# Moving the left operands of three matmul stages to other addresses relative to their weights

## The chip, the cores and the metric

The kernel runs on one core of a Trainium2 chip. The metric is device time in microseconds (us) of one execution. Before the change three runs took 2002.62, 2002.87 and 2003.62 us, median 2002.87.

## The reference

One decoder layer on 256 tokens of width 2048, in float32: half a SwiGLU feed-forward (FFN), a mixer (eight retention heads beside eight gated-delta heads, one input and one output projection), another half FFN, and a final RMSNorm.

```python
x = x + 0.5 * _swiglu(_rmsnorm(x, norm_ffn1_w[l]), ffn1_w_gate[l], ffn1_w_up[l], ffn1_w_down[l])
x = x + _mixer(_rmsnorm(x, norm_mix_w[l]), positions, w_in[l], ..., w_out[l])
x = x + 0.5 * _swiglu(_rmsnorm(x, norm_ffn2_w[l]), ffn2_w_gate[l], ffn2_w_up[l], ffn2_w_down[l])
return _rmsnorm(x, norm_final_w)
```

The weights are 2048 x 5632 (gate, up), 5632 x 2048 (down), 2048 x 8208 (mixer in) and 2048 x 2048 (mixer out).

## The kernel before

All products are done in float32 quality by splitting both operands into a high and a low part (type fp32r) and adding three matmuls, `triple` (lines 144 to 151): left high by weight high, left high by weight low, left low by weight high. A matmul has a stationary left operand of 128 x 128 (`lhsT`, loaded by an LDWEIGHTS) and a moving right operand of 128 x 512, which is the piece of weights. The next LDWEIGHTS runs while the present matmul streams.

Weights come by DMA in pieces of 256 rows x 512 columns (`raw`); ScalarE casts the high part (`whi`, line 135), VectorE subtracts for the low part (`wlo`, line 136). `whi` and `wlo` are pools of four buffers each, used by all stages. The last four pieces of the second FFN have buffers of their own (pool `wlast`, `KEPT` = 4).

The left operands are, by stage:

- gate and up of both FFNs and the mixer's input projection: `xh`, `xl`, the transposed, normalised activations, kept for the whole kernel;
- the down projections of the two FFNs: `hh`, `hl` (lines 327, 328), in a pool that each FFN opens anew. A down projection is done in two halves, of 6 and of 5 blocks of 512 rows;
- the mixer's output projection: four pairs named `m8`, `mh4`/`ml4`, `mh0`/`ml0`, `mh12`/`ml12`, which take over buffers of the pool `gd` (line 476).

The order of the instructions on TensorE (PE), VectorE (DVE) and ScalarE (ACT) is written out by hand. In the mixer, side chains on the same engines (convolutions, gates, the delta rule, retention) are run between the matmuls of the input projection.

The three pools that hold left operands are laid out one behind the other in each partition of SBUF, so a dummy tile at a pool's start shifts all that follows in it. Before the change there are two such pads, of 8 floats (32 bytes): in the first FFN's pool and in `gd`. Every slice that a matmul reads starts at a multiple of 512 bytes behind its tile's start, so a stage has one distance between left operand and weights modulo 256.

Of the kernel before, what the change touches and what calls it, by code (L numbers as in the profile page):

```python
# [13 lines left out]
F32 = mybir.dt.float32  # L14
# [5 lines left out]
P = 128  # L20
# [9 lines left out]
Q = 32  # L30
KEPT = 4
LEAD = 3
PAD = 8
NLEV = 7
HALF = P // 2
LEV0 = 5
# [49 lines left out]
def hybrid_layer(ctx: ExitStack, tc: tile.TileContext, a: dict, out: bass.AP):  # L86
# [99 lines left out]
    def product_units(left, w, rows, c0, sizes=()):  # L186

        accs = [acc.tile([P, NB], F32, name="acc") for _ in range(NT)]

        def units():
            for ks, _ in product_pieces(rows, w, c0, sizes):
                hi, lo = stream.take((w.tensor.name, c0), len(ks))
                for j, k in enumerate(ks):
                    for t in range(NT):
                        triple(accs[t], left, rows[k][0], t, hi[:, j, :], lo[:, j, :], k == 0, k == len(rows) - 1)
                        yield

        return accs, units()

    def staggered_product(left, w, rows, c0, kept):


        accs = [acc.tile([P, NB], F32, name="acc") for _ in range(NT)]
        pieces = list(product_pieces(rows, w, c0))
        split_pieces = {}

        def piece(i, t):  # L210
            if t == 0:
                split_pieces[i] = stream.take((w.tensor.name, c0), len(pieces[i][0]))
            hi, lo = split_pieces[i]
            for j, k in enumerate(pieces[i][0]):
                triple(accs[t], left, rows[k][0], t, hi[:, j, :], lo[:, j, :], k == 0, k == len(rows) - 1)

        lag = 2
        stream.lead = 1
        for i in range(len(pieces)):
            piece(i, 0)  # L220
            if i == 0:
                do_later()
            if lag <= i < len(pieces) - kept:
                piece(i - lag, 1)
        yield accs[0]
        for i in range(len(pieces) - kept - lag, len(pieces)):
            piece(i, 1)
        yield accs[1]
# [13 lines left out]
    def product(*args, every=2):  # L242
        accs, units = product_units(*args)
        beside(units, every)
        return accs
# [4 lines left out]
    def vector_transposed(dst, src):  # L250


        dv = dst.rearrange("p n (t c) -> p t n c", t=NT)
        sv = src.rearrange("p t (n c) -> p t n c", c=P)

        def piece(r):
            for q in range(0, P, Q):
                V.transpose(dv[q:q + Q, :, :, r:r + Q], sv[r:r + Q, :, :, q:q + Q])  # L258

        return [partial(piece, r) for r in range(0, P, Q)]  # L260
# [24 lines left out]
    def norm_block(ssq, i, b, xt=None):  # L285


        kb = NB // P
        ks = range(b * kb, (b + 1) * kb)

        def squares():
            for t in range(NT):
                square_sum(ssq, b, t)

        if xt is None:
            return [partial(norm_pair, i, k) for k in ks[::2]] + [squares]
        return (vector_transposed(xt, x[:, :, b * NB:(b + 1) * NB]) + [partial(norm_tile, i, k, xt[:, k - ks[0], :]) for k in ks]
                + [squares])
# [5 lines left out]
    def row_factor(ssq):  # L304
        w = ssq.shape[1]
        r = small.tile([P, w], F32, name="rms")
        V.tensor_reduce(r, ssq, mybir.AxisListType.X, ALU.add)
        V.tensor_scalar(r, r, 1.0 / D, EPS, ALU.mult, ALU.add)
        q = small.tile([P, w], F32, name="rfac")
        power(q, r, -0.5, w)  # L310
        return q

    def ffn(idx, factor, after, lead=None):


        wg, wu, wd = a[f"ffn{idx}_w_gate"][0], a[f"ffn{idx}_w_up"][0], a[f"ffn{idx}_w_down"][0]
        nblk, nout = FF // NB, D // NB
        halves = [range(0, (nblk + 1) // 2), range((nblk + 1) // 2, nblk)]
        kb = NB // P
        rf = None  # L320
        with (tc.manual_schedule(engines={E.PE, E.DVE, E.Activation}), tc.tile_pool(name=f"ffn{idx}", bufs=1) as hp, tc.tile_pool(name=f"ffe{idx}", bufs=1) as ep,
              tc.tile_pool(name=f"wlast{idx}", bufs=KEPT) as wl):
            pools["last"] = wl
            if idx == 1:

                hp.tile([P, PAD], F32, name="pad")
            hh = hp.tile([P, len(halves[0]) * kb, T], F32R, name="hh")
            hl = hp.tile([P, len(halves[0]) * kb, T], F32R, name="hl")

            def h_left(k):  # L330
                return hh[:, k, :], hl[:, k, :]

            for hf in halves:
                rows = [(k, k) for k in range(KD)]
                for i, b in enumerate(hf):
                    u = None
                    if b == 0 and lead:
                        g, gs = product_units(x_left, wg, rows, 0, (1, 1))
                        u, us = product_units(x_left, wu, rows, 0)
                        for k in range(0, KD, 2):  # L340
                            lead(k, ep)
                            for units in (gs, us):
                                deque(islice(units, 2 * NT), 0)
                            stream.lead = 1
                        stream.lead = LEAD
                    else:
                        g = product(x_left, wg, rows, b * NB)
                    if rf is None:
                        rf = factor()
                    sg = ep.tile([P, NT, NB], F32, name="sg", bufs=4 - idx)  # L350
                    for t in range(NT):
                        S.activation(sg[:, t, :], g[t], AF.Silu, scale=rf[:, t:t + 1])  # L352
                    u = u or product(x_left, wu, rows, b * NB)
                    h = ep.tile([P, NT, NB], F32, name="h", bufs=4 - idx)
                    for t in range(NT):
                        V.scalar_tensor_tensor(h[:, t, :], u[t], rf[:, t:t + 1], sg[:, t, :], ALU.mult, ALU.mult)
                    ht = ep.tile([P, kb, T], F32, name="ht")
                    later.extend(vector_transposed(ht, h))
                    for j in range(0, kb, 2):
                        ks = slice(i * kb + j, i * kb + j + 2)  # L360
                        later.append(partial(split, hh[:, ks, :], hl[:, ks, :], ht[:, j:j + 2, :]))
                r0 = hf[0] * kb
                rows = [(k, r0 + k) for k in range(len(hf) * kb)]
                last = hf is halves[1]
                for b in range(nout):
                    if last and idx == 2 and b == nout - 1:
                        o = staggered_product(h_left, wd, rows, b * NB, KEPT)
                    else:
                        o = product(h_left, wd, rows, b * NB)
                    for t, ot in enumerate(o):  # L370
                        xs = x[:, t, b * NB:(b + 1) * NB]
                        V.scalar_tensor_tensor(xs, ot, 0.5, xs, ALU.mult, ALU.add)
                        if last:
                            after(b, t, ep)
# [93 lines left out]
    def first_factor():  # L468
        for t in range(NT):
            square_sum(ssqs[0], D // NB - 1, t)  # L470
        return row_factor(ssqs[0])

    ffn(1, first_factor, to_mixer, start)


    with tc.manual_schedule(engines={E.PE, E.DVE, E.Activation}), tc.tile_pool(name="gd", bufs=1) as gd:
        gd.tile([P, PAD], F32, name="pad")

        def mixed_out(o, b, xt=None):
            for t in range(NT):  # L480
                xs = x[:, t, b * NB:(b + 1) * NB]
                V.tensor_tensor(xs, o[t], xs, ALU.add)
            later.extend(norm_block(ssqs[2], 2, b, xt))

        env = dict(x_left=x_left, ident=ident, mx=mx, cv=cv, qd=qd, product=product, product_units=product_units, power=power,
                   split=split,
                   weight_piece=weight_piece, do_later=do_later, beside=beside, mixed_out=mixed_out,
                   row_factor=lambda: row_factor(ssqs[1]), params=(cst, alog, dtb, gnw, cw, posi))
        mixer(tc, a, gd, env)
# [659 lines left out]
```

## Time and profile before

| | |
|---|---|
| median of three runs | 2002.87 us |
| the profiled execution | 2002.66 us |
| its span, first to last instruction | 2000.8 us |
| PE busy | 1966.6 us, 98% |
| LDWEIGHTS (PEld) busy | 1618.0 us, 81% |
| DVE busy | 1289.9 us, 64% |
| ACT busy | 892.4 us, 45% |
| granted TensorE clock, mean | 0.997 |

Time outside the span is 1.9 us. A matmul's recorded duration is longer than the distance to the next matmul's start, since matmuls are pipelined: "busy" says that PE has one under way, and the distance from start to start says what one costs. The stages follow each other: first FFN to about 727 us, mixer to about 1272 us, second FFN to the end.

### The profile page before, as it was taken

The numbers are of one execution on the slowest core, as the hardware profiler recorded it, in microseconds if no ns is written. First come the engines' busy times: TensorE is split into PE (matmuls) and PEld (weight loads), VectorE is DVE, ScalarE is ACT, GpSimd is POOL, SyncE is SP. The second block draws the span as 40 slices with busy tenths as digits, with TensorE's granted clock in tenths as the row PEclk, the third lists the DMA queues.
The fourth block names the chain that finished last, engine by engine and source line by source line (L and its number), as shares of the span: only waits on it lengthen the run. The fifth ranks groups of instructions, "written<-read, shape, count | busy, mean of one in ns | idle before, by whom it ended". The sixth has DMA issues, their size and how long they took to land.

```text
span 2000.8 us, 23620 instructions
## 1 busy us (share of the span) xinstructions
PE 1966.6 (98%) x8836; PEld 1618.0 (81%) x8836; DVE 1289.9 (64%) x1818; ACT 892.4 (45%) x1075; POOL 61.8 (3%) x79
## 2 busy tenths in 40 slices
PE   9999999999999999999999999999999999999998
PEld 7888888888888887877777788888888888888886
DVE  5676664457666777676568567766676544677654
ACT  6444443343444456644344334544444334444443
POOL 0000000000000000120121000000000000000000
PEclk9999999999999999999999999999999999999999
DMA  9565655665565565586557835666665656665564
GB/s 313 190 190 180 208 197 193 193 197 182 188 208 193 190 188 169 160 172 162 124 152 170 165 122 184 206 200 194 195 189 179 210 193 196 191 195 182 189 208 139
DMA packets 195267, 373.06 MB, mean 186 GB/s; under 512 B 14544, under 2 KB 15184, under 8 KB 195024
## 3 DMA queue, kind: packets, MB, share of 16 engines
q1 hardware_dynamic: 193888, 368.38, 60.3%
q0 software_dynamic: 832, 1.84, 0.4%
q8 instruction: 69, 1.13, 0.2%
q10 hardware_dynamic: 432, 1.34, 0.2%
q14 instruction: 46, 0.38, 0.1%
HBM read 368.89 MB, written 2.62 MB: 186 GB/s over the span
## 4 chain that ended last, share of the span: by engine, by line
PE 48%; DVE 4%; issue 1%; ACT 1%; DMA 0%; POOLq 0%; DVEq 0%; ACTq 0%
PE acc L149 15%; PE acc L151 15%; PE acc L150 15%; DVE wlo L136 1%; ACT whi L135 1%; PE mx L748 1%; PE qd L828 0%; DVE yn L857 0%; DVE Yb L858 0%; DMA raw<-in_ffn_w_down_dram 0%; DVE rv L1056 0%; PE mx L1025 0%; DVE gu L769 0%; PE mx L979 0%; PE mx L811 0%
## 5 line engine op out<-in xcount | busy, mean ns | idle before, releaser
L136 DVE TENSOR_TENSOR wlo<-raw,whi 128x1024 fp32r<-128x1024 f32 (+1 forms) x689 | 840.4, 1227 | 623.0 <-ACT whi L135 620.1
L135 ACT CAST whi<-raw 128x1024 fp32r<-128x1024 f32 (+1 forms) x689 | 720.3, 1051 | 818.3 <-PE acc L151 741.7
L149 PE MATMUL acc<-whi,xh 128*128 128x512 f32 x1920 | 762.1, 397 | 1.6 <-DVE xl L273 1.6
L150 PE MATMUL acc<-wlo,xh 128*128 128x512 f32 x1920 | 750.3, 391 | 1.2 <-DVE wlo L136 1.2
L151 PE MATMUL acc<-whi,xl 128*128 128x512 f32 x1920 | 750.2, 391 | 0.0
L151 PEld LDWEIGHTS acc<-whi,xl 128*128 128x128 f32 x1920 | 361.6, 188 | 76.2
L149 PEld LDWEIGHTS acc<-whi,xh 128*128 128x128 f32 x1920 | 362.4, 189 | 74.6 <-ACT whi L135 2.7
L150 PEld LDWEIGHTS acc<-wlo,xh 128*128 128x128 f32 x1920 | 362.2, 189 | 74.1 <-DVE wlo L136 3.1
L150 PE MATMUL acc<-wlo,hh 128*128 128x512 f32 x704 | 274.0, 389 | 0.2 <-DVE wlo L136 0.2
L149 PE MATMUL acc<-whi,hh 128*128 128x512 f32 x704 | 273.9, 389 | 0.0
L151 PE MATMUL acc<-whi,hl 128*128 128x512 f32 x704 | 273.9, 389 | 0.0
L258 DVE STREAM_TRANSPOSE ht<-h 32x256 f32<-32x256 f32 x352 | 153.3, 436 | 5.3
L150 PEld LDWEIGHTS acc<-wlo,hh 128*128 128x128 f32 x704 | 132.1, 188 | 28.2 <-DVE wlo L136 0.7
L149 PEld LDWEIGHTS acc<-whi,hh 128*128 128x128 f32 x704 | 132.1, 188 | 27.5
L151 PEld LDWEIGHTS acc<-whi,hl 128*128 128x128 f32 x704 | 132.1, 188 | 27.3
L141 ACT CAST hh<-ht 128x512 fp32r<-128x512 f32 x44 | 27.2, 617 | 121.2 <-DVE ht L258 121.2
L142 DVE TENSOR_TENSOR hl<-ht,hh 128x512 fp32r<-128x512 f32 x44 | 30.3, 688 | 15.1 <-ACT hh L141 15.1
L352 ACT ACTIVATE sg<-acc,rfac 128x512 f32<-128x512 f32 x44 | 29.9, 690 | 19.3 <-PE acc L151 16.6
L149 PE MATMUL acc<-whi,mh 128*128 128x512 f32 x96 | 37.7, 393 | 0.0
L151 PE MATMUL acc<-whi,ml 128*128 128x512 f32 x96 | 37.4, 390 | 0.0
L150 PE MATMUL acc<-wlo,mh 128*128 128x512 f32 x96 | 37.4, 389 | 0.0
L726 DVE SCALAR_TENSOR_TENSOR y<-cv,cw,y 128x255 f32<-128x255 f32 (+2 forms) x72 | 34.6, 480 | 3.0 <-ACT y L718 1.2
(215 smaller groups left out, 762.2 us busy)
## 6 DMA issues: line engine op xcount, KB each, us to landing
raw<-in_ffn_w_up_dram SPq DMA_DIRECT2D x176, 512.0 KB, 4.5
raw<-in_ffn_w_down_dram SPq DMA_DIRECT2D x176, 512.0 KB, 4.6
raw<-in_ffn_w_gate_dram SPq DMA_DIRECT2D x175, 512.0 KB, 4.3
raw<-in_w_in_dram SPq DMA_DIRECT2D x128, 512.0 KB, 4.8
raw<-in_w_out_dram SPq DMA_DIRECT2D x32, 512.0 KB, 3.5
x<-in_x_dram SPq DMA_DIRECT2D x4, 512.0 KB, 6.3
out_dram<-x SPq DMA_DIRECT2D x8, 256.0 KB, 2.4
h<-in_xt_dram SPq DMA_DIRECT2D x7, 256.0 KB, 5.9
```

The source lines that it names most:

```text
L135: S.copy(hi, raw)
L136: V.tensor_tensor(lo, raw, hi.bitcast(F32), ALU.subtract)
L141: S.copy(hi, src)
L142: V.tensor_tensor(lo, src, hi.bitcast(F32), ALU.subtract)
L149: PE.matmul(o, lhsT=sh, rhs=hi, start=first, stop=False)
L150: PE.matmul(o, lhsT=sh, rhs=lo, start=False, stop=False)
L151: PE.matmul(o, lhsT=sl, rhs=hi, start=False, stop=last)
L258: V.transpose(dv[q:q + Q, :, :, r:r + Q], sv[r:r + Q, :, :, q:q + Q])
L352: S.activation(sg[:, t, :], g[t], AF.Silu, scale=rf[:, t:t + 1])
L726: V.scalar_tensor_tensor(yy[:, lag:], pt[:, j, :T - lag], w[:, 3 - lag:4 - lag], yy[:, lag:], ALU.mult, ALU.add)
L748: PE.matmul(pt[:, j, :], lhsT=lhsT, rhs=rhs, start=True, stop=True)
```

## The change

The first FFN's pad grows from 8 to 56 floats, the second FFN gets one of 16 floats, the mixer's is taken out.

```diff
-PAD = 8
...
-            if idx == 1:
-
-                hp.tile([P, PAD], F32, name="pad")
+
+            hp.tile([P, 56 if idx == 1 else 16], F32, name="pad")
             hh = hp.tile([P, len(halves[0]) * kb, T], F32R, name="hh")
...
     with tc.manual_schedule(engines={E.PE, E.DVE, E.Activation}), tc.tile_pool(name="gd", bufs=1) as gd:
-        gd.tile([P, PAD], F32, name="pad")
```

No instruction is added, taken out or moved, and no wait changes: the two programs have the same instructions in the same order with the same semaphores on every engine. Only addresses differ. Byte addresses within a partition, modulo 256:

| tiles | before | after |
|---|---|---|
| `whi`, `wlo`, `xh`, `xl`, `raw`, `x` | 160 | 160 |
| `hh`, `hl`, `h`, `sg`, `ht` of the first FFN | 160 | 96 (64 below the weights) |
| `hh`, `hl`, `h`, `sg`, `ht` of the second FFN | 160 | 224 (192 below, or 64 above) |
| `whi`, `wlo` of the last four pieces | 160 | 224 (as `hh`, `hl`) |
| `m8`, `mh4`, `ml4` and the others; `kq`, `gu`, `kd` and all of `gd` | 160 | 128 (32 below) |
| `rkT`, `rqT`, `sc`, `rv`, `rg` | 32 | 0 |
| `slr` | 0 | 224 |
| `pe`, `y`, `sq` | 224 | 192 |
| `ident` | 128 | 128 |

## Rows read from the trace of the kernel before

**Rows 1.** The page, parts 1 and 2: engines' busy time; granted clock by slice.

```profile
PE 1966.6 (98%) x8836; PEld 1618.0 (81%) x8836; DVE 1289.9 (64%) x1818; ACT 892.4 (45%) x1075; POOL 61.8 (3%) x79
...
PEclk9999999999999999999999999999999999999999
```

**Rows 2.** The page, part 4: the chain that ended last, shares by line.

```profile
PE acc L149 15%; PE acc L151 15%; PE acc L150 15%; DVE wlo L136 1%; ACT whi L135 1%; PE mx L748 1%; PE qd L828 0%; DVE yn L857 0%; DVE Yb L858 0%; DMA raw<-in_ffn_w_down_dram 0%; DVE rv L1056 0%; PE mx L1025 0%; DVE gu L769 0%; PE mx L979 0%; PE mx L811 0%
```

**Rows 3.** Windows: stretch, length, busy (instructions), granted clock, DMA share, GB/s.

```profile
280.00:400.00 120.00, 120.00 (x531) 99.38 (x530) 61.48 (x58) 48.30 (x47) 0.00 (x0) 1.00 0.59 194
...
1680.00:1880.00 200.00, 200.00 (x884) 165.59 (x883) 127.58 (x154) 86.61 (x91) 0.00 (x0) 1.00 0.61 194
```

**Rows 4.** One tile's instructions in a stretch: count, ns min/median/max, first and last start.

```profile
L149 PE MATMUL acc<-whi,hh x192: 389/389/389, 270.4 to 400.3; 128*128 128x512 f32 x192
...
L149 PE MATMUL acc<-whi,xh x320: 389/389/389, 401.0 to 617.9; 128*128 128x512 f32 x160
...
L149 PE MATMUL acc<-whi,hh x192: 389/389/389, 1534.6 to 1664.4; 128*128 128x512 f32 x192
```

**Rows 5.** Groups by line on PE: count, busy us, mean ns, idle before.

```profile
L149 PE MATMUL acc<-whi,hh 128*128 128x512 f32 x704 | 273.9, 389 | 0.0
...
L149 PE MATMUL acc<-whi,mh 128*128 128x512 f32 x96 | 37.7, 393 | 0.0
...
L149 PE MATMUL acc<-whi,m 128*128 128x512 f32 x32 | 12.6, 395 | 0.0
```

**Rows 6.** The page, part 5: the casts that feed the matmuls.

```profile
L136 DVE TENSOR_TENSOR wlo<-raw,whi 128x1024 fp32r<-128x1024 f32 (+1 forms) x689 | 840.4, 1227 | 623.0 <-ACT whi L135 620.1
L135 ACT CAST whi<-raw 128x1024 fp32r<-128x1024 f32 (+1 forms) x689 | 720.3, 1051 | 818.3 <-PE acc L151 741.7
```

**Rows 7.** Timeline in the mixer: start us, us, engine, line, operation.

```profile
805.58 0.14 PEld L716 LDWEIGHTS cv<-ident,pe 128*128 128x128 f32 x1
...
824.91 0.39 PE L151 MATMUL acc<-whi,xl 128*128 128x512 f32 x1
824.92 0.19 PEld L773 LDWEIGHTS mx<-gu,slr 128*128 128x128 f32 x1
825.14 0.40 PE L773 MATMUL mx<-gu,slr 128*128 128x512 f32 x1
...
832.30 0.48 PEld L736 LDWEIGHTS mx<-ident,kq 128*128 128x128 f32 x3
...
843.03 0.41 PEld L811 LDWEIGHTS mx<-kq 128*128 128x128 f32 x2
...
973.41 0.53 PEld L748 LDWEIGHTS mx<-w,kd 128*128 128x128 f32 x3
...
1044.00 0.42 PEld L1034 LDWEIGHTS mx<-rv,sc 128*128 128x128 f32 x2
```

**Rows 8.** The matmul that streams over each of those loads, columns as in rows 4.

```profile
L151 PE MATMUL acc<-whi,xl x1: 392/392/392, 805.6 to 805.6; 128*128 128x512 f32 x1
...
L151 PE MATMUL acc<-whi,xl x1: 391/391/391, 824.9 to 824.9; 128*128 128x512 f32 x1
...
L151 PE MATMUL acc<-whi,xl x1: 392/392/392, 832.3 to 832.3; 128*128 128x512 f32 x1
...
L151 PE MATMUL acc<-whi,xl x1: 389/389/389, 843.0 to 843.0; 128*128 128x512 f32 x1
...
L151 PE MATMUL acc<-whi,xl x1: 389/389/389, 973.4 to 973.4; 128*128 128x512 f32 x1
...
L151 PE MATMUL acc<-whi,xl x1: 392/392/392, 1044.0 to 1044.0; 128*128 128x512 f32 x1
```

**Rows 9.** The tile `slr` in the stretch 1011 to 1012 us, columns as in rows 4.

```profile
L773 PE MATMUL mx<-gu,slr x2: 391/392/393, 1011.4 to 1011.7; 128*128 128x512 f32 x2
```

**Rows 10.** Window of the 32 gate matmuls of 256 columns (tile `wab`), columns as in rows 3.

```profile
738.40:742.10 3.70, 3.67 (x32) 3.37 (x32) 0.00 (x0) 0.00 (x0) 1.00 0.54 159
```

## The prediction

> **What bounds the kernel now.** I read the page's busy times first: PE is busy 98% of the span at full clock, DVE 64%, ACT 45% [rows 1]. The chain that ended last is led by the three matmul lines of `triple` in equal shares; nothing else reaches 2% [rows 2]. So the time is the number of matmuls times the distance from one start to the next. The windows of pure stages give that distance: a window counts every matmul that touches it, so (length + one duration) / count is (120 + 0.389) / 531 = 226.7 ns in a down projection and (200 + 0.389) / 884 = 226.7 ns in gate and up [rows 3]. The tiles' first and last starts say the same: (400.3 - 270.4) / 191 / 3 = 226.7 ns for `hh` in the first FFN, 226.6 for `xh`, 226.5 in the second FFN, each good to about 0.2 ns [rows 4]. The reader is to see a single number in all stages, and in all of them left operand and weights are at the same address modulo 256. The recorded duration is 389 ns in each, without spread [rows 4]: duration minus distance is 162 ns, so one ns more in the duration can be read as about one ns more in the distance, finer than the timeline's 10 ns.
>
> 226.7 ns is 544 cycles of 2.4 GHz for 512 columns. That columns stream one per cycle follows from the 256-column matmuls: 3.7 us / 32 = 116 ns, and (226.7 - 116) / 256 = 0.43 ns per column against 0.417 for a cycle [rows 10]. So 512 columns need 213.3 ns, and 13.3 ns of each matmul are something else, perhaps the LDWEIGHTS that runs beside it.
>
> **The change part by part.** No instruction, order or wait changes, so the only term is the distance in the matmuls whose left operand moves. Their count: `hh` has 704 matmuls on line 149 and as many on each of the other two lines, 2112 in all, half in each FFN [rows 5]; the mixer's output projection has 96 + 32 per line, 384 in all [rows 5]. The last four pieces of the second FFN have weights that move with `hh`: 8 blocks of 128 rows x 2 token tiles x 3 = 48 matmuls stay at distance zero. So 1056 matmuls go to 64 below, 1008 to 192 below, 384 to 32 below: 2448 of the kernel's big ones. The `xh`/`xl` stages don't move.
>
> The trace of before has no such matmul in a steady stage; it has single ones in the mixer, where a big matmul (weights at 160) streams while the next, small one's left operand is loaded from elsewhere [rows 7]. With `kq` and `kd` (160, distance zero) the big one took 389 ns, as in the steady stages [rows 8]. With `slr` (at 0, which is 160 below) it took 391 [rows 8]; that is the one pair of the same form as the steady ones, fp32r and 128 x 128, and two further matmuls around it that load or stream from `slr` and `gu` took 391 and 393 [rows 9]. With `sc` (at 32, 128 below) it took 392 [rows 8]. Against this stand the transposes: loading `pe` (224, 192 below) gave 392, but loading `kq` for a transpose (160, distance zero) gave 392 as well [rows 7, 8], so for this kind the address shows nothing and there is 3 ns of another origin.
>
> That bounds the cost per matmul: 0 ns (the pair of transposes, equal at distance zero and at 192 below) to +3 ns (`sc` against `kq`) on the side of a loss. On the side of a gain the bound is the whole 13.3 ns, for no row shows distances 64 and 32 in this form. I take a value between by distance: zero at 0, +3 at 128 below, and in a straight line between, back to zero at 256. At 160 that gives 2.25, and `slr` measured 2. It gives 1.5 ns at 64, 1.5 at 192 and 0.75 at 32. The sum: 1056 x 1.5 = 1.6 us, 1008 x 1.5 = 1.5 us, 384 x 0.75 = 0.3 us; together 3.4 us.
>
> The Trainium skill, "TensorE: Matmul & The Clock Gate", Part 2, in the step on LDWEIGHTS, says that the moving operand and the weight load have a read port each, so that the load takes no read bandwidth from the running matmul. By that rule no address could matter and the sum would be 0; the rows with 391 and 392 ns speak against it, the pair of transposes for it.
>
> What else moves: the mixer's own 580 small matmuls (8836 - 8256), most of whose operands shift together; at +/- 1.5 ns this is 0.9 us at most. DVE and ACT work on shifted tiles, but each has slack: a piece of weights takes DVE 1227 ns and ACT 1051 ns [rows 6] against 12 matmuls of 226.7 = 2720 ns. This slack is also the cover if PE became faster: at 213.3 ns a piece would still leave PE the slowest, at 2560 ns. DMA shares stay as they are, since `raw` does not move.
>
> The sum against the profiled execution: 2002.66 + 3.4 = 2006.1 us; the median of the runs stands 0.2 us above that execution, so the forecast is 2006.3 us. The differences on which it rests are 2 to 3 ns in a handful of records, so it is weak.
>
> **The rivals.** Nothing happens: the 2 to 3 ns belong to the change from a big matmul to a small one and not to the address. For it: the transposes show such a difference at distance zero. Against it: `kq` and `kd` show none at distance zero. Time 2002.9, with a us either way.
>
> It becomes faster: the 13.3 ns are the load's reads meeting the stream's, because both start at the same address modulo 256, and another distance keeps them apart. For it: the excess exists, is the same in all stages, and all stages share the distance. Against it: 160 and 128 below show no shorter matmul than 389 [rows 8, 9]. Price if all three distances were clean: 2448 x 13.3 = 32.6 us, 1970; if only 64 or only 192 below is, about 13.4 to 14.0 us, 1989; if only 32 below is, 5.1 us, 1998. The same page, under "Phases on the wall clock", gives a gap of about 216 ns for 512 columns; by that figure the estimate would be 10.9 ns a matmul, 26.7 us, 1976. The trace disagrees with the figure in every stage, 226.7.
>
> It becomes clearly slower: at a short distance the load's reads run close to the stream's and meet it all along, where at 0 and at 128 or 160 they part. For it: the excess at zero may already be such meetings, and 32 and 64 are not in the trace. Against it: 2 to 3 ns is all that the trace shows of any distance. Price from 4 ns for all 2448 (9.8 us, 2012.7) to a second 13.3 ns for the two short distances (1440 x 13.3 = 19.2 us, 2022). It decides from 1.7 ns a matmul on, 4.1 us.
>
> That the pads don't shift what they say is excluded by the addresses; the 48 matmuls above are the exception.
>
> **How the numbers follow.** The forecast's case, 2004 to 2010 us, has 0.38; nothing 0.25; faster 0.20; clearly slower 0.17. A measurement of this kernel tells about 0.2% (4 us) from no change, that is 2006.9 and 1998.9. Somewhat over half of the forecast's case lies within (0.22), as does all of nothing and 0.03 of faster (only 32 below clean and the like): 0.50. Slower: 0.16 + 0.17 = 0.33. Faster: 0.17. The range from 1997.5 to 2013 leaves out the larger gains (0.12) and the larger losses (0.08).
>
> **What would show it.** In the windows of rows 3 the count in 280 to 400 us falls from 531 to 527 or 528 if a down projection's matmul takes 228.2 ns; it stays at 531 if nothing happens, and rises to 564 at 213.3. The `hh` duration goes from 389 to 390 or 391. The `xh` row must stay at 389 and 226.7: if it moves too, it is not the distance. The three stages apart give the three distances: the straight line is wrong if the mixer's 32 below costs more than the 64 of the first FFN, or if 192 below differs from 64 below by over 1 ns. The prediction is wrong in its base if any stage gets faster.

## The result and the profile after

The changed kernel takes 2013.7 us (median of four runs, 2012.98 to 2014.09) against 2002.8 of the kernel before in the same job: ratio 1.0053, interval 1.0036 to 1.0071. It is slower, by 10.9 us. The profiled execution took 2013.77 us with a span of 2012.0, 11.2 us more than before's 2000.8.

The page of the changed kernel answers [rows 1, 2]: PE is busy for 98% at full clock with the same 8836 matmuls, DVE and ACT did the same work in the same time, and the chain has the same three lines in front (`triple` is now on lines 148 to 150; lines stand one lower there and three lower in the mixer).

```profile
PE 1976.6 (98%) x8836; PEld 1617.1 (80%) x8836; DVE 1290.7 (64%) x1818; ACT 891.7 (44%) x1075; POOL 61.6 (3%) x79
...
PEclk9999999999999999999999999999999999999999
...
PE acc L148 15%; PE acc L149 15%; PE acc L150 15%; DVE wlo L135 1%; ACT whi L134 1%; PE mx L745 1%; PE qd L825 0%; DMA raw<-in_ffn_w_down_dram 0%; DMA raw<-in_w_in_dram 0%; DVE yn L854 0%; DVE gu L766 0%; DVE rv L1053 0%; DVE Yb L855 0%; PE mx L1022 0%; PE mx L976 0%
```

So no wait came in. What changed is how many matmuls fit into a stretch. These are the windows of the first FFN's down projection, the second FFN's, the mixer's output projection and gate and up; columns as in [rows 3]:

```profile
280.00:400.00 120.00, 120.00 (x526) 98.44 (x525) 61.06 (x57) 47.23 (x47) 0.00 (x0) 1.00 0.62 193
...
1540.00:1660.00 120.00, 120.00 (x516) 96.70 (x515) 64.30 (x67) 45.69 (x46) 0.00 (x0) 1.00 0.59 188
...
1240.00:1275.00 35.00, 35.00 (x152) 28.12 (x151) 30.59 (x50) 19.39 (x29) 0.00 (x0) 1.00 0.62 195
...
1680.00:1880.00 200.00, 200.00 (x884) 165.65 (x883) 127.56 (x154) 86.60 (x91) 0.00 (x0) 1.00 0.65 194
```

(Length + one duration) / count is (120 + 0.392) / 526 = 228.9 ns at 64 below, (120 + 0.395) / 516 = 233.3 ns at 192 below, and still 226.7 ns, 884 matmuls, in gate and up, whose operands didn't move against each other. The mixer's window is short and gives 232.9; its starts over 10 us of the timeline (1261.80 to 1271.84, 43 distances) give 233.5, and a longer stretch (1213.50 to 1276.50, 270 distances) 233.3. The same stages by tile, beside [rows 4]:

```profile
L148 PE MATMUL acc<-whi,hh x192: 392/392/392, 270.4 to 401.6; 128*128 128x512 f32 x192
L149 PE MATMUL acc<-wlo,hh x192: 394/394/394, 270.6 to 401.8; 128*128 128x512 f32 x192
L150 PE MATMUL acc<-whi,hl x192: 388/388/389, 270.9 to 402.0; 128*128 128x512 f32 x192
...
L148 PE MATMUL acc<-whi,xh x320: 389/389/389, 402.3 to 619.2; 128*128 128x512 f32 x160
...
L148 PE MATMUL acc<-whi,hh x192: 393/396/398, 1538.8 to 1672.5; 128*128 128x512 f32 x192
```

The first half of the first down projection went from 129.9 us between first and last start to 131.2, that of the second from 129.8 to 133.7; the stretch of `xh` takes 216.9 us in both. The sum over the program, with each stage's distance: 1056 x 2.2 = 2.4 us, 1008 x 6.7 = 6.7 us, 384 x 6.7 = 2.6 us, together 11.7, of 11.2 measured in the span. The difference lies in the mixer's output projection, which took 93.9 us from first to last start (1182.6 to 1276.5) against 91.9 (1180.4 to 1272.3): 2.0 us and not 2.6; small matmuls and a wait lie between its big ones. The price doesn't come and go with the casts: DVE is busy for 61 of the 120 us at 64 below and ACT for 47, and all 192 records of line 148 have 392 ns. Nor does the load itself get longer; an LDWEIGHTS takes 187 or 188 ns in these stages, as before. The groups of [rows 5] are longer now:

```profile
L148 PE MATMUL acc<-whi,hh 128*128 128x512 f32 x704 | 277.1, 394 | 0.0
...
L148 PE MATMUL acc<-whi,mh 128*128 128x512 f32 x96 | 38.3, 399 | 0.0
```

The timeline shows what the means hide. Start in us, duration in us, engine, line: first 64 below, then 192 below, then the program's last matmuls, whose weights moved along with `hh` so that their distance is zero.

```profile
299.95 0.39 PE L148 MATMUL acc<-whi,hh 128*128 128x512 f32 x1
300.18 0.39 PE L149 MATMUL acc<-wlo,hh 128*128 128x512 f32 x1
300.41 0.39 PE L150 MATMUL acc<-whi,hl 128*128 128x512 f32 x1
300.63 0.39 PE L148 MATMUL acc<-whi,hh 128*128 128x512 f32 x1
...
1599.92 0.40 PE L149 MATMUL acc<-wlo,hh 128*128 128x512 f32 x1
1600.16 0.39 PE L150 MATMUL acc<-whi,hl 128*128 128x512 f32 x1
1600.39 0.40 PE L148 MATMUL acc<-whi,hh 128*128 128x512 f32 x1
1600.63 0.39 PE L149 MATMUL acc<-wlo,hh 128*128 128x512 f32 x1
...
2001.16 0.39 PE L148 MATMUL acc<-whi,hh 128*128 128x512 f32 x1
...
2002.52 0.39 PE L148 MATMUL acc<-whi,hh 128*128 128x512 f32 x1
```

At 64 below the steps are 230, 230, 220 in the view's 10 ns (averaged over the stage 229, 232 and 226, 687 per triple). At 192 below they alternate, 240, 230, 240 (averaged 236 and 231). At distance zero six matmuls take 1.36 us, 226.7 each. The matmuls run in a repeating pattern, and a pattern's mean is the price. In cycles of 2.4 GHz the means are 544, 549.3 and 560.

### The profile page after: what moved, and what is told of

Read it like the earlier page. It is cut to its first block, busy times and chain, and to the rows that moved or that the text cites. A ratio compares the mean times of both kernels' runs of the same rounds, so it can differ in the third digit from the quotient of the medians.

```text
span 2012.0 us, 23620 instructions
## 1 busy us (share of the span) xinstructions
PE 1976.6 (98%) x8836; PEld 1617.1 (80%) x8836; DVE 1290.7 (64%) x1818; ACT 891.7 (44%) x1075; POOL 61.6 (3%) x79
## 4 chain that ended last, share of the span: by engine, by line
PE 48%; DVE 3%; issue 1%; ACT 1%; DMA 1%; POOLq 0%; DVEq 0%; ACTq 0%
PE acc L148 15%; PE acc L149 15%; PE acc L150 15%; DVE wlo L135 1%; ACT whi L134 1%; PE mx L745 1%; PE qd L825 0%; DMA raw<-in_ffn_w_down_dram 0%; DMA raw<-in_w_in_dram 0%; DVE yn L854 0%; DVE gu L766 0%; DVE rv L1053 0%; DVE Yb L855 0%; PE mx L1022 0%; PE mx L976 0%
## 5 line engine op out<-in xcount | busy, mean ns | idle before, releaser
L135 DVE TENSOR_TENSOR wlo<-raw,whi 128x1024 fp32r<-128x1024 f32 (+1 forms) x689 | 841.2, 1228 | 633.0 <-ACT whi L134 630.0
L134 ACT CAST whi<-raw 128x1024 fp32r<-128x1024 f32 (+1 forms) x689 | 719.4, 1049 | 832.8 <-PE acc L150 754.0
```

The source lines that it names most:

```text
L134: S.copy(hi, raw)
L135: V.tensor_tensor(lo, raw, hi.bitcast(F32), ALU.subtract)
```

## The experiments

Questions: is it the distance between left operand and weights, or the stage, or the left operand's own address; is the straight line by distance right; can a distance be found that is better than zero. All kernels below are the kernel before with other pads (before has 8, none, 8): `PAD[1]` and `PAD[2]` are floats ahead of `hh` in the two FFNs, `PADM` floats at the start of `gd`, and `SLIP`, where it is named, floats from the start of the tiles `hh` and `hl` to the first used one. Of each edit only the lines that set the distances are shown. The runs of one job share the kernel before, whose median was 2004.3, 2003.6 and 2003.9 us in the three jobs; where only one run was timed, the verdict is read from the stages in its trace, each good to about 0.2 ns.

**The three distances go round** (192, 32 and 64 below in the first FFN, the second and the mixer).

```diff
-PAD = 8
+PAD = {1: 24, 2: 56}
+PADM = 56
```

> The same three distances dealt to other stages: first FFN's down projection 192 below the weights modulo 256, second FFN's 32 below, mixer's output projection 64 below. Theory A (the distance sets the price): 233.3 ns per matmul in the first FFN, 233.3 in the second, 228.9 in the mixer, so 1056 x 6.67 + 1008 x 6.67 + 384 x 2.2 = 14.6 us over before, about 2017.4 us. Theory B (the stage sets it, by its other buffers or its evictions): 228.9 in the first FFN, 233.3 in the second and in the mixer, as in the changed kernel, about 2013.7 us.

Measured: 2014.88 us against 2004.31, ratio 1.0059 (1.0036 to 1.0082). The tile `hh` in the two FFNs and `mh` in the mixer:

```profile
L151 PE MATMUL acc<-whi,hh x192: 393/396/398, 270.7 to 404.4; 128*128 128x512 f32 x192
...
L151 PE MATMUL acc<-whi,hh x192: 393/395/397, 1540.5 to 1674.2; 128*128 128x512 f32 x192
...
L151 PE MATMUL acc<-whi,mh x41: 394/394/394, 1244.7 to 1277.7; 128*128 128x512 f32 x41
```

The first FFN now has (404.4 - 270.7) / 573 = 233.3 ns, the second 233.3, and the mixer 228.9 (1261.67 to 1271.97, 45 distances). The price went with the distance; that it belongs to the stage is refuted. The distances give 1056 x 6.6 + 1008 x 6.6 + 384 x 2.2 = 14.5 us; the span (2013.0) is 12.2 over before's 2000.8. Of the 2.3 us missing, 2.0 lie in the mixer ahead of its output projection: from the first matmul of `xh` there to the first of `mh` the trace shows 1194.4 - 727.4 = 467.0 us before and 1199.7 - 734.7 = 465.0 here. That stretch, with its side chains between the matmuls, varies from kernel to kernel (466.9 in the changed one, 467.4 with all tiles moved by 64 bytes); which of its tiles does it wasn't tried.

**The own address.** All tiles move by 64 bytes, so that all distances stay zero, at address 224.

```diff
+    const.tile([P, 16], F32, name="allpad")
```

> All of x, xh, xl, raw, whi, wlo, hh, hl and the mixer's tiles 64 bytes higher, every distance zero as before, every address 224 modulo 256 instead of 160. Theory A (distance alone): 226.7 ns in all stages, 2002.8 us. Theory D (the left operand's own address: 224 is where the second FFN's operands lie in the changed kernel): 233.3 ns for the 8256 big matmuls, 55 us more, about 2058 us.

Measured: 2002.72 us (eight runs) against 2004.31, ratio 0.9991 (0.998 to 1.0003), no difference. First `hh`, then `xh`:

```profile
L152 PE MATMUL acc<-whi,hh x192: 389/389/389, 271.5 to 401.3; 128*128 128x512 f32 x192
...
L152 PE MATMUL acc<-whi,xh x320: 389/389/389, 402.0 to 618.9; 128*128 128x512 f32 x160
```

Both have 226.7 ns. An address of 224 cost 6.7 ns a matmul in the changed kernel's second FFN, where the weights were at 160, and costs nothing here. It is the distance.

**One part undone.** The second FFN goes back to zero, the others stay as in the change.

```diff
-PAD = 8
+PAD = {1: 56, 2: 0}
+PADM = 0
```

> The changed kernel without the second FFN's pad: first FFN 64 below, second FFN at distance zero, mixer 32 below. If the stages' costs add up, the second FFN's 1008 matmuls x 6.67 ns = 6.7 us come back: about 2007.0 us, and 226.7 ns in that stage, with 228.9 and 233.3 left in the other two. If what one stage loses is not simply its own (a queue or a buffer handed on), the time stays nearer to 2013.7.

Measured: 2007.31 us (ten runs) against 2003.6, ratio 1.0015 (1.0006 to 1.0025): 3.7 us more (the interval is 1.2 to 5.0), where the changed kernel has 10.9. `hh` in the two FFNs:

```profile
L151 PE MATMUL acc<-whi,hh x192: 392/392/392, 270.5 to 401.7; 128*128 128x512 f32 x192
...
L151 PE MATMUL acc<-whi,hh x192: 389/389/389, 1538.0 to 1667.9; 128*128 128x512 f32 x192
```

The first FFN keeps its 229 ns and the second is back at 226.7; the two stages left come to 1056 x 2.2 + 384 x 6.7 = 4.9 us by count. The stages add up within the noise; over half of the loss is the second FFN's 192 below.

**Other distances** (96, 128 and 160 below).

```diff
+PAD = {1: 48, 2: 32}
+PADM = 32
```

> Distances not yet seen: 96 below (first FFN), 128 below (second FFN), 160 below (mixer). The prediction's straight line, scaled to the 6.67 ns at 192, would have its highest price at 128, over 10 ns, and about the same at 96 and 160. Theory A with steps: each stage at one of few values, 226.7, 228.9, 233.3 ns or the like, in multiples of a third of 16 cycles (2.2 ns), without order by distance. Theory C (both streams meet more often at zero than elsewhere): some distance falls below 226.7 ns.

Measured: 2016.5 us (one run).

```profile
L151 PE MATMUL acc<-whi,hh x192: 394/394/394, 270.6 to 404.3; 128*128 128x512 f32 x192
...
L151 PE MATMUL acc<-whi,hh x192: 390/393/404, 1542.7 to 1675.8; 128*128 128x512 f32 x192
...
L151 PE MATMUL acc<-whi,mh x43: 392/397/400, 1244.8 to 1279.9; 128*128 128x512 f32 x43
```

96 below has 233.3 ns, 128 below 232.4 (starts 1542.65 to 1676.28, 575 distances), 160 below 234.3 (1217.11 to 1280.37, 270 distances). The line that rises to a peak at 128 is refuted: 128 is not the worst, and 96 costs three times as much as 64.

**Short distances on both sides** (16 below, 16 above, 224 below).

```diff
+PAD = {1: 0, 2: 0}
+SLIP = {1: 4, 2: 4}
+PADM = 16
```

> Distances 16 below (first FFN), 16 above (second FFN), 32 above, which is 224 below (mixer). If the price depends on the sign, 16 below and 16 above differ; if only on closeness, both are alike and 32 above costs as 32 below, 233.3 ns. If a step of 16 bytes is too small to matter, both FFNs stay at 226.7 ns.

Measured: 2004.63 us (one run). First `hh` in each FFN, then `mh`, then a part of the last half of the second FFN:

```profile
L151 PE MATMUL acc<-whi,hh x192: 389/389/389, 270.2 to 400.1; 128*128 128x512 f32 x192
...
L151 PE MATMUL acc<-whi,hh x192: 389/389/389, 1536.5 to 1666.4; 128*128 128x512 f32 x192
...
L151 PE MATMUL acc<-whi,mh x34: 395/396/396, 1245.0 to 1273.7; 128*128 128x512 f32 x34
...
L151 PE MATMUL acc<-whi,hh x48: 388/394/396, 1960.2 to 1992.7; 128*128 128x512 f32 x48
```

16 bytes to either side cost nothing at first, and 224 below, which is 32 above, costs 6.7 ns like 32 below. The last row is the catch: same distance as the second, but after an irregularity in the stream the stage goes on with a median of 394 ns and with 233.3 ns from start to start. The irregularity is one late load: it began 0.11 us after the matmul beside it, where the others begin within 0.01, just behind the end of the subtraction that makes the low part its own matmul streams (1969.81 us before). The kernel before has it at the same place. First before, then this run:

```profile
1969.76 0.39 PE L149 MATMUL acc<-whi,hh 128*128 128x512 f32 x1
1969.87 0.19 PEld L150 LDWEIGHTS acc<-wlo,hh 128*128 128x128 f32 x1
...
1971.71 0.39 PE L151 MATMUL acc<-whi,hh 128*128 128x512 f32 x1
1971.82 0.19 PEld L152 LDWEIGHTS acc<-wlo,hh 128*128 128x128 f32 x1
```

Before, at distance zero, is back at 226.7 ns after some eight matmuls; 16 above does not come back by the end. So the same distance can have two pitches, and which one runs depends on what came before. At distance zero no stage of any run stayed slow after an irregularity.

**Distances in steps of 16** (48 and 112; 176 and 208; 80 and 144; the mixer at zero).

```diff
+PAD = {1: 56, 2: 32}
+SLIP = {1: 4, 2: 4}
```

> Odd multiples of 16: 48 below (first FFN), 112 below (second FFN), mixer at zero. If 16 bytes are one step of what matters, these lie between their neighbours or at 226.7 as 16 below did; if pairs of 32 bytes are the step, 48 is as 32 (233.3) or 64 (228.9) and 112 as 96 (233.3) or 128 (232.4). A value under 226.7 would make a faster kernel than before.

```diff
+PAD = {1: 24, 2: 8}
+SLIP = {1: 4, 2: 4}
```

> 176 below (first FFN), 208 below (second FFN), mixer at zero. Neighbours: 160 gave 234.3 ns, 192 and 224 gave 233.3. If all distances but zero and 16 to either side cost 2.2 to 7.6 ns, both stages lie between 228.9 and 234.3. A value under 226.7 would make a faster kernel than before.

```diff
+PAD = {1: 48, 2: 24}
+SLIP = {1: 4, 2: 4}
```

> 80 below (first FFN), 144 below (second FFN), mixer at zero. If the free distances are zero with 16 to either side and 112 alone, both cost 2 to 7.6 ns a matmul. If they lie 128 apart (112 and 0 with a slip of 16), 144, which is 128 below 16, is free at 226.7 ns and 80 is not.

Measured: 2009.5, 2013.48 and 2014.15 us (one run each). `hh` at 48 and 112 below, and at 80 and 144 below:

```profile
L151 PE MATMUL acc<-whi,hh x192: 395/396/397, 270.7 to 403.5; 128*128 128x512 f32 x192
...
L151 PE MATMUL acc<-whi,hh x192: 389/389/389, 1541.4 to 1671.3; 128*128 128x512 f32 x192
```

```profile
L151 PE MATMUL acc<-whi,hh x192: 387/391/398, 271.5 to 403.3; 128*128 128x512 f32 x192
...
L151 PE MATMUL acc<-whi,hh x192: 394/394/394, 1539.6 to 1673.3; 128*128 128x512 f32 x192
```

48 has 231.9 ns, 112 has 226.7, 80 has 230.0 and 144 has 233.3; 176 and 208 have 232.0 and 233.3. 112 is free, its mirror image 144 is not, so the price is not symmetric about zero. 112 too went over to longer distances near the end of its last half, after the same late load (mean of that half 228.0 ns).

**Below 16 bytes** (8 and 4 below).

```diff
+PAD = {1: 0, 2: 56}
+SLIP = {1: 6, 2: 7}
```

> Distances of less than 16 bytes: 8 below (first FFN), 4 below (second FFN), mixer at zero. If steps of 16 bytes are what matters, 8 and 4 below behave as zero or as 16 below, both 226.7 ns. If a word's own place matters, they may cost anything from 226.7 to 234; below 226.7 is possible only if the excess at zero is not needed.

Measured: 2007.59 us (one run).

```profile
L151 PE MATMUL acc<-whi,hh x192: 393/396/397, 269.1 to 402.8; 128*128 128x512 f32 x192
...
L151 PE MATMUL acc<-whi,hh x192: 389/389/390, 1539.5 to 1669.4; 128*128 128x512 f32 x192
```

8 bytes below cost the full 6.7 ns, 4 bytes nothing, and 16 nothing. So the price doesn't go by blocks of 16 bytes either. The weights of the second FFN's last four pieces follow the pad but not the slip, so in the runs with a slip the left operands of these 48 matmuls lie the slip above them, whatever the stage's distance. Here that is 28 above (228 below), and they ran at 233 ns.

All distances, in ns per matmul, by bytes below the weights modulo 256:

| 0 | 4 | 8 | 16 | 32 | 48 | 64 | 80 | 96 |
|---|---|---|---|---|---|---|---|---|
| 226.7 | 226.7 | 233.3 | 226.7 | 233.3 | 231.9 | 228.9 | 230.0 | 233.3 |

| 112 | 128 | 144 | 160 | 176 | 192 | 208 | 224 | 240 |
|---|---|---|---|---|---|---|---|---|
| 226.7 | 232.4 | 233.3 | 234.3 | 232.0 | 233.3 | 233.3 | 233.3 | 226.7 |

None is below 226.7, so no kernel came out that beats the one before. That these are distances modulo 256 and not a longer period is borne out by before itself, where `hh` was at other multiples of 256 in the two FFNs at one price, and by 192 below, which has 233.3 ns in both FFNs. For the other distances it wasn't tried. A period of 128 is excluded, since 64 and 192 differ.

**The greatest stages.** `xh` and `xl` are put 32 below, everything else stays at zero: the pad stands behind them in their pool, so all that is laid out after them moves up by 32 bytes.

```diff
+    keep.tile([P, 8], F32, name="xpad")
```

> xh and xl, the left operands of gate, up and the mixer's input projection (5760 matmuls), 32 bytes below the weights; all other distances zero. Theory A (the distance sets the price for whichever operand): 233.3 ns in their stages, 5760 x 6.67 = 38 us more, about 2041 us, somewhat less where the mixer's small matmuls lie between. If it belongs to the operands that are written late (hh, hl and the mixer's are written by ScalarE and VectorE shortly before they are read; xh and xl are too in the first FFN, but lie still in later blocks), the stages of gate and up stay at 226.7 ns and the time at 2003.

Measured: 2035.34 us (two runs) against 2003.93, ratio 1.0154 (1.0125 to 1.0184).

```profile
L152 PE MATMUL acc<-whi,xh x320: 393/395/397, 409.0 to 632.3; 128*128 128x512 f32 x160
...
L152 PE MATMUL acc<-whi,hh x192: 389/389/390, 278.4 to 408.3; 128*128 128x512 f32 x192
```

The stretch of `xh` between first and last start grew from 216.9 to 223.3 us, a factor of 1.030 as 233.3 / 226.7 is, and `hh` stays at 226.7. So the distance sets the price for these tiles too, which feed most of the kernel's matmuls. 31.4 us more is under the some 37 us forecast. The shortfall lies in the mixer: its input projection, with the side chains between the big matmuls, took 457.5 us from first to last start (741.8 to 1199.3) against 452.4 (727.4 to 1179.8), 5.1 us more, where 1536 x 6.67 would be 10.2.

**Which of the two left operands.** In the first FFN `hh` is at zero and `hl` 32 below, in the second `hh` is 32 below and `hl` at zero.

```diff
+            hp.tile([P, PAD_HH[idx]], F32, name="pad")
             hh = hp.tile([P, len(halves[0]) * kb, T], F32R, name="hh")
+            hp.tile([P, PAD_HL[idx]], F32, name="pad2")
             hl = hp.tile([P, len(halves[0]) * kb, T], F32R, name="hl")
```

> High and low left operand apart. First FFN: hh at zero, hl 32 below. Second FFN: hh 32 below, hl at zero. Mixer at zero. Theory A1 (a load disturbs the matmul that streams beside it, which is the one before its own): with hl displaced the matmul on the line of weight low (streams while hl loads) is the long one; mean per matmul (2 x 226.7 + 233.3) / 3 = 228.9 in the first FFN and (226.7 + 2 x 233.3) / 3 = 231.1 in the second. Theory A2 (a matmul suffers from its own left operand's place): the same means, with the last matmul of the triple long in the first FFN. If the pattern depends on the run of several matmuls, the means are other than these.

Measured: 2015.21 us (one run). The three lines of the triple in the first FFN, then in the second:

```profile
L151 PE MATMUL acc<-whi,hh x192: 389/389/389, 270.2 to 402.7; 128*128 128x512 f32 x192
...
L152 PE MATMUL acc<-wlo,hh x192: 396/396/396, 270.5 to 402.9; 128*128 128x512 f32 x192
...
L153 PE MATMUL acc<-whi,hl x192: 394/394/394, 270.7 to 403.1; 128*128 128x512 f32 x192
...
L151 PE MATMUL acc<-whi,hh x192: 394/397/397, 1540.2 to 1673.9; 128*128 128x512 f32 x192
...
L152 PE MATMUL acc<-wlo,hh x192: 397/397/397, 1540.4 to 1674.1; 128*128 128x512 f32 x192
...
L153 PE MATMUL acc<-whi,hl x192: 393/393/397, 1540.7 to 1674.4; 128*128 128x512 f32 x192
```

From start to start the three are 226.7, 235.0 and 231.7 ns in the first FFN. The longest is that of line 152: beside its stream the displaced `hl` is loaded. That fits theory A1. But the one after it pays as well, though the load beside it is at distance zero, and the second FFN doesn't fit: there the displaced `hh` is loaded beside lines 153 and 151, and the three are 236, 233 and 231 ns for lines 151, 152 and 153, the shortest with a displaced load beside it. So neither theory is shown; which matmul of a triple pays can't be told from its load alone. The mean in the first FFN is 231.1 ns instead of the 228.9 that one displaced load in three would give by addition; the second FFN, with two of three, has 233.3, as with all three. The price belongs to the pattern of several matmuls.

**Half a load.** In the down projections, matmuls that are in neither the first nor the last triple of their sum load and compute 64 of the 128 columns of the left operand, so half of the tokens' sums are left out; first FFN 32 below, second and mixer at zero.

```diff
+        if left.__name__ == "h_left" and not first and not last:
+            o, sh, sl = o[:HALF], sh[:, :HALF], sl[:, :HALF]
```

> In the down projections the left operand has 64 columns instead of 128 in all but the first and last triple of a sum, so half of the tokens' sums are left out; the streams keep their 512 columns. First FFN 32 below, second FFN and mixer at zero. If the excess over 213.3 ns (512 cycles) comes from the reads of the load, half a load has half the excess: 220.0 ns (528 cycles) in the second FFN, where a full load has 226.7, and 223.3 (536) in the first, where it has 233.3. If it is a fixed cost of each matmul, 226.7 and 233.3 remain.

Measured: 2011.65 us (one run). `hh` in the first FFN, then in the second:

```profile
L153 PE MATMUL acc<-whi,hh x192: 390/393/398, 270.3 to 402.7; 128*64 128x512 f32 x176, 128*128 128x512 f32 x16
...
L153 PE MATMUL acc<-whi,hh x192: 389/389/398, 1540.5 to 1672.1; 128*64 128x512 f32 x176, 128*128 128x512 f32 x16
```

Both expectations fell. The distance of starts is 231.1 ns at 32 below (less than 233.3) and 229.7 at zero (more than 226.7). So the 13.3 ns above 512 columns are not a share of the load's length, since they don't halve with it. The full loads (16 of 192 on a line) don't explain it: in an unbroken stretch of half loads at zero (1544.82 to 1571.95, 118 distances) the mean is 229.9. What the 13.3 ns are stays open.

## Why the prediction was wrong

The time, 2013.7, lies above the forecast of 2006.3 and just above the range's end of 2013; slower by over 0.2% had a chance of 0.33.

- **One term decides, the distance of starts.** Right. Same count, same clock, same chain; gate and up stayed at 884 matmuls in 200 us, and the price followed the distance wherever a run moved it.
- **The price by distance.** This is the step that failed: "I take a value between by distance: zero at 0, +3 at 128 below, and in a straight line between, back to zero at 256." It gave 1.6 us for 64 below (measured 2.4), 1.5 for 192 below (6.7) and 0.3 for 32 below (2.6 by count and distance, 2.0 in the trace). In its place the runs show a price without order by distance, 2.2 ns at 64 below and 6.7 at 192 and 32. Both tests set beforehand came out against it: the mixer's 32 costs more than the first FFN's 64, and 192 differs from 64 by 4.4 ns. There is no slope by distance at all in the table: 4 and 16 are free, 8 and 32 are not.
- **Reading it from single records.** The rows with 391 and 392 ns [rows 8, 9] pointed the right way: the address does count. But `slr`, 160 below, showed +2 ns, and a stage at 160 below has 234.3 - 226.7 = 7.6. A single displaced load among loads at zero is not a stage of them: the displaced load in three of the run with `hl` alone already cost two matmuls, 8.3 and 5.0 ns.
- **Duration for distance.** Right. "One ns more in the duration can be read as about one ns more in the distance" holds even line by line, to about 2 ns: at 64 below the three lines have 392, 394 and 388 ns for steps of 229, 232 and 226, and in the second FFN with `hh` alone displaced 397, 397 and 393 for 236, 233 and 231. What misled was not this reading but the few records that it was applied to.
- **The other small terms.** DVE and ACT took the same time per piece (1228 and 1049 ns against 1227 and 1051 in [rows 6]), so the shifted tiles cost them nothing.
- **Rivals.** Nothing, 2002.9: refuted. Faster: refuted for the 17 other distances tried, none under 226.7. Clearly slower: its lower price, 4 ns for all 2448 and 2012.7 us, was 1.0 us under the result, but that is luck: the split is another (2.2, 6.7 and 6.7), and its reason, that short distances collide while long ones part, is refuted: 192 costs as much as 32, and 64 less than 96.
- **The rule of the page.** The Trainium skill, "TensorE: Matmul & The Clock Gate", Part 2, says that the load has a read port of its own and takes no bandwidth from the running matmul. The runs disagree with its consequence for the time: the address of a load relative to the streamed weights moves the distance by up to 7.6 ns at the same instructions. Whether read bandwidth is what is lost isn't shown.

What is shown: distance modulo 256 between the left operand that is loaded and the weights that stream sets the mean pitch of a stage, and at 16 above and 112 below what came before decides between two of them. Why these distances are free and those not, and what the 13.3 ns at distance zero are, wasn't settled by any run.

## What to carry to other kernels

In a kernel that is bound by back-to-back matmuls with a load each, look at the addresses: tiles of left operands and of streamed operands that start at the same address modulo 256 ran at 226.7 ns a matmul here, most other distances 1 to 3% slower, and a small tile that is put into a pool anywhere ahead can change that without moving one instruction. Read the pitch stage by stage, as (window + one duration) / count, since busy shares don't show it: PE was 98% busy before and after. And don't price a steady stage from an isolated record; a run of one stage at the new layout was needed.

## What was not expected

- Distances can be free and yet not safe: 16 above and 112 below ran at 226.7 ns through a whole half and went on at some 233 ns after one load that came 0.1 us late, while zero recovered each time.
- 8 bytes cost 6.7 ns where 4 and 16 cost nothing.
- Halving the loaded columns made the matmul at distance zero slower, 229.7 against 226.7 ns, though a load was shorter, 0.13 to 0.14 us against 0.19 in the timeline.
